# All of TensorE's work in one written order: wide and narrow products in twos, the second column pair one unit behind

## The chip, the core and the metric

The kernel runs on one core of a Trainium2 chip. The metric is the device time of one execution, in microseconds (us), shorter being better. The engines that matter are TensorE (PE, matrix products, with its weight loads on a lane of its own, PEld), VectorE (DVE), ScalarE (ACT) and SyncE (SP), whose queue issues nearly all DMAs.

## The reference

A trunk of four residual layers over 256 tokens of width 2048, in float32: a state-space mixer (SSD), a gated FFN, a short gated convolution, and another gated FFN, with an RMS norm ahead of each and one at the end.

```
for i in range(DEPTH):                       # DEPTH = 2
    h = rms_norm(x, mix_norm_w[i])
    x = x + (ssd_mixer(h, ...) if i % 2 == 0 else short_conv_mixer(h, ...))
    h = rms_norm(x, ffn_norm_w[i])
    x = x + conv_ffn(h, ...)                 # (silu(g) * v) @ w_down, (g, v) = conv(h @ w_up)
return rms_norm(x, final_norm_w)
```

The mixer has 8 groups. For a group it needs the columns xs and z of `h @ w_in`, a matrix of decays m (exponentials of differences of a running sum, times the product of C and B), y = m · (dt · xs) + D · xs, then y · silu(z), an RMS norm over the 512 channels of the group, and the product with w_out.

## The kernel before

**Precision.** Every float32 product is made of three products of a reduced type (float32r). A weight w is split into wh = round(w), a cast on ScalarE (L287), and wl = w − wh, a subtraction on VectorE (L288). An activation is split in the same way into the two halves of a tile `hl` (L217, L218): 256 columns of high parts, then 256 of low ones. The **wide** product (L334) multiplies wh with all 512 columns of `hl`, the **narrow** product (L335) multiplies wl with the 256 high ones. In the mixer's xs and bc streams (`one=True`) the wide product is made as two narrow ones (L331, L332), so that all three add into the same 256 columns.

**Units and streams.** All weight matrices are read as a list of units of 2 × 128 rows by 512 columns (512 KB, `plan`). A unit goes through one of 4 `raw` buffers (the DMA) and one of `WB` = 4 pairs of wh and wl. `stream` (L308) takes one set of 512 output columns: for each unit it takes the four 128-column tiles t and for each t the two k, a wide and then a narrow product. Column tiles 0 and 1 add up in one PSUM buffer, 2 and 3 in another (the two column pairs; there are 3 such buffers, `main`). When the last unit is done, `evac(0)` and `evac(1)` take the two buffers out.

**Side work on TensorE.** Small products and transposes go through two further PSUM buffers (`aux`): the transposes of x at the start (L421), those of ten rows of parameters (L149, `turn_params`), the product that gives dt (L513) and the running sums (L547 to L555); for each mixer group cb (L597), the transposes of xs (L630), the y products (L649, L657), the sum over channels for the norm (L194, fed by `one`, L680) and the broadcast of the norm factor (L187); and the same two for each layer's norm.

**Order.** Each engine runs its own list of instructions from front to back. The kernel's code names the work and what depends on what; where an instruction stands in an engine's list is worked out by a scheduler when the kernel is built, except where `pin` keeps instructions in program order (the startup: `x_pair` as a hook inside the first stream).

**Stages in the profiled execution.** The startup and first stream run to 37 us, dt at about 60, the first xs stream from about 67 and the first z stream from 94.5, then seven more mixer groups; SSD output products, the first FFN from about 700, the short convolution from about 1460, the second FFN from about 1830. In the second FFN the products with w_down (L858 to L860) are three wide products of another form; the change doesn't touch them.

Of the kernel before, what the change touches and what calls it, by code (L numbers as in the profile page):

```python
# [8 lines left out]
F32 = mybir.dt.float32  # L9
# [7 lines left out]
P = 128  # L17
# [22 lines left out]
def trunk_kernel(ctx, tc, a, out):  # L40
    nc = tc.nc
    mm = nc.tensor.matmul
# [16 lines left out]
    n_id = [0]  # L59

# [86 lines left out]
    def turn_params(i, rt, n, put=lambda ins: ins):  # L147
        ps = aux()
        put(nc.tensor.transpose(ps[:, :n], rt[:n, :], ident[:n, :n]))  # L149
        put(nc.vector.tensor_copy(prm[i][:, :n], ps[:, :n]))  # L150
# [31 lines left out]
    def bcast_tok(r, dg=None):  # L182

        dg = dg or diag_tok(r)
# [112 lines left out]

    def weight_unit(c0, kc, ahead=WB - 1):

        i = taken[0]  # L300
        assert plan[i][1:] == (c0, kc), (plan[i], c0, kc)
        taken[0] += 1
        while len(units) < min(i + ahead + 1, len(plan)):
            load_unit()
        got, units[i] = units[i], None
        return got

    def stream(c0, hls, kcs, evac, one=False, before=None):  # L308
# [6 lines left out]
        put = (lambda ins: ins) if before is None else pin  # L315
        for u in range(0, n, KU):
            order = [(t, k) for t in range(4) for k in range(KU)]
            if before is not None and u == 0:
                before(0)
                order.sort(key=lambda tk: tk[1])  # L320
            wh, wl = weight_unit(c0, kcs[u], WB - 1 if before is None else 0)
            for at, (t, k) in enumerate(order):
                if before is not None and at == (0 if u else 2) and u + KU < n:
                    before(u // KU + 1)
                i = u + k
                o = pts[t // 2][:, t % 2, :]
                hl = hls[i // 2][:, i % 2, :]
                lw = slice(t * P, (t + 1) * P)
                first, last = i == 0, i == n - 1
                if one:  # L330
                    put(mm(o[:, 0:T], wh[:, k, lw], hl[:, 0:T], start=first, stop=False))  # L331
                    put(mm(o[:, 0:T], wh[:, k, lw], hl[:, T : 2 * T], start=False, stop=False))  # L332
                else:
                    put(mm(o, wh[:, k, lw], hl, start=first, stop=False))  # L334
                put(mm(o[:, 0:T], wl[:, k, lw], hl[:, 0:T], start=False, stop=last))  # L335
        if before is not None:
            before(n // KU)
        if taken[0] < len(plan):
            while len(units) < min(taken[0] + WB - 1, len(plan)):
                load_unit()  # L340
# [36 lines left out]
    class Norm:  # L377
# [15 lines left out]
        def row(self):  # L393
            one = small.tile([P, T], F32, tag="nacc1", name=uid("nacc1"))
            tt(out=one, in0=self.acc[:, 0, :], in1=self.acc[:, 1, :], op=ALU.add)
            r = mean_rsqrt(tok_sum(one), D)
            ps = bcast_tok(r)
            rb = small.tile([P, T], F32, tag="rrow", name=uid("rrow"))
            nc.scalar.copy(rb, ps)
            return rb  # L400
# [7 lines left out]
    def x_pair(m):  # L408
        if m == NKD // 2:
            for i in range(1, 4):  # L410
                turn_params(i, *prows[i - 1], pin)
            ps = bcast_tok(first["r_tok"], first["dg"])
# [3 lines left out]
            return  # L416
        ps = aux()
        for j in range(2):
            for c in range(2):
                k = 2 * m + j  # L420
                pin(nc.tensor.transpose(  # L421
                    ps[:, j * T + c * P : j * T + (c + 1) * P], xt[:, c, k * P : (k + 1) * P], ident
                ))
        if m:
            load_unit()
        t = xpool.tile([P, 2, T], F32, tag="x", name=uid("x"))
        copy = nc.vector.tensor_copy if m < 2 else nc.scalar.copy
        pin(copy(t, ps.rearrange("p (j t) -> p j t", j=2)))
        xp.append(t)
        h = new_hl()  # L430
        xhl.append(h)
        if m == 0:
            turn_params(0, *prow0, pin)
# [22 lines left out]
    def bc_stream(g, o, before=None):  # L456
# [10 lines left out]
        stream(2 * DI + o * NG * DS + g * DS, xhl, range(NKD), evac, True, before)  # L467
# [42 lines left out]
    ps = aux()  # L510
    for c in range(2):
        for k in range(NKD):
            mm(  # L513
                ps[:, c * NH : (c + 1) * NH], xp[k // 2][:, k % 2, c * P : (c + 1) * P],
                dtw[:, k, :], start=(k == 0), stop=(k == NKD - 1),
            )
    NT = 2 * NH

    def st(tag):
        return tokpool.tile([P, NT], F32, tag=tag, name=tag, bufs=1)  # L520

    v, e, t1, t2, q_ = st("dt_v"), st("dt_e"), st("dt_t1"), st("dt_t2"), st("dt_q")
    for c in range(2):
        stt(
            out=v[:, c * NH : (c + 1) * NH], in0=ps[:, c * NH : (c + 1) * NH],
            scalar=r_tok[:, c : c + 1], in1=bias_bc, op0=ALU.mult, op1=ALU.add,
        )
    na = tokpool.tile([P, NH], F32, tag="na", name="na", bufs=1)
    pin(act(na, alog_bc, AF.Exp))
    act(e, v, AF.Abs)  # L530
    act(e, e, AF.Exp, scale=-1.0)
    ts(out=t1, in0=e, scalar1=2.0, scalar2=None, op0=ALU.add)
    nc.vector.reciprocal(t1, t1)
    tt(out=t1, in0=t1, in1=e, op=ALU.mult)
    tt(out=t2, in0=t1, in1=t1, op=ALU.mult)
    ts(out=q_, in0=t2, scalar1=1.0 / 17.0, scalar2=None, op0=ALU.mult)
    for k in (15, 13, 11, 9, 7, 5, 3):
        stt(out=q_, in0=q_, scalar=1.0 / k, in1=t2, op0=ALU.add, op1=ALU.mult)
    stt(out=q_, in0=q_, scalar=1.0, in1=t1, op0=ALU.add, op1=ALU.mult)
    ts(out=v, in0=v, scalar1=0.0, scalar2=None, op0=ALU.max)  # L540
    dt = cpool.tile([P, 2, NH], F32, tag="dt", name="dt")
    stt(out=dt.rearrange("p c h -> p (c h)"), in0=q_, scalar=2.0, in1=v, op0=ALU.mult, op1=ALU.add)
    da = tokpool.tile([P, 2, NH], F32, tag="da", name="da", bufs=1)
    for c in range(2):
        stt(out=da[:, c, :], in0=dt[:, c, :], scalar=-1.0, in1=na, op0=ALU.mult, op1=ALU.mult)
    ps = aux()
    mm(ps[:, 0:NT], triu, da.rearrange("p c h -> p (c h)"), start=True, stop=True)  # L547
    cs = cpool.tile([P, 2, NH], F32, tag="cs", name="cs")
    nc.vector.tensor_copy(cs.rearrange("p c h -> p (c h)"), ps[:, 0:NT])
    ps = aux()  # L550
    mm(ps[:, 0:NH], ones, da[:, 0, :], start=True, stop=True)
    rem = cpool.tile([P, NH], F32, tag="rem", name="rem")
    tt(out=rem, in0=ps[:, 0:NH], in1=cs[:, 0, :], op=ALU.subtract)
    ps = aux()
    nc.tensor.transpose(ps[:, 0:P], cs.rearrange("p c h -> p (c h)"), ident)  # L555
    cst = tokpool.tile([P, P], F32, tag="cst", name="cst", bufs=1)
    nc.scalar.copy(cst, ps[:, 0:P])
    cs_d = dpool.tile([2, NH, P], F32, tag="cs_d", name="cs_d")
    nc.scalar.dma_start(out=cs_d.rearrange("c h l -> (c h) l"), in_=cst)
# [353 lines left out]
```

## Time and profile before

| | us |
|---|---|
| median of 3 runs | 2562.86 (2562.57 to 2566.78) |
| the profiled execution, whole | 2563.32 |
| its span in the profile | 2561.5 |
| ACT busy | 1321.5 (52%) |
| weight loads (PEld) busy, beside PE | 2235.2 (87%) |

Busy times of PE, DVE, ACT and PEld overlap each other. The row of a matrix product gives a duration that includes its passage through the array, and one product starts long before the one ahead has ended. So the pace of TensorE is read from start to start, or from the count of products in a stretch without idle time, and not from the mean duration. In brackets behind a row stands the idle time of the engine just ahead of it, and what ended it. The granted TensorE clock of the whole execution was 0.998 of full speed. The DMA engines moved 187 GB/s on the mean.

### The profile page before, as it was taken

The numbers are of one execution on the slowest core, as the hardware profiler recorded it, in microseconds if no ns is written. First come the engines' busy times: TensorE is split into PE (matmuls) and PEld (weight loads), VectorE is DVE, ScalarE is ACT, GpSimd is POOL, SyncE is SP. The second block draws the span as 40 slices with busy tenths as digits, with TensorE's granted clock in tenths as the row PEclk, the third lists the DMA queues.
The fourth block names the chain that finished last, engine by engine and source line by source line (L and its number), as shares of the span: only waits on it lengthen the run. The fifth ranks groups of instructions, "written<-read, shape, count | busy, mean of one in ns | idle before, by whom it ended". The sixth has DMA issues, their size and how long they took to land.

```text
span 2561.5 us, 38324 instructions
## 1 busy us (share of the span) xinstructions
PE 2544.6 (99%) x15101; PEld 2235.2 (87%) x15101; DVE 1790.2 (70%) x2601; ACT 1321.5 (52%) x1630; POOL 1.1 (0%) x8
## 2 busy tenths in 40 slices
PE   9999999999999999999999999999999999999998
PEld 9999998998888888888888888888888888888886
DVE  7888876788677776557776666666677774577765
ACT  5565643566555554345554444444555553455543
POOL 0000000000000000000000000000000000000000
PEclk9999999999999999999999999999999999999999
DMA  7666655665666665666665666666566666666664
GB/s 229 175 184 193 182 176 188 189 182 172 198 183 191 190 188 181 193 188 183 193 190 181 193 186 185 185 197 189 174 183 187 189 197 190 193 186 188 189 192 145
DMA packets 255737, 478.76 MB, mean 187 GB/s; under 512 B 17668, under 2 KB 29124, under 8 KB 255428
## 3 DMA queue, kind: packets, MB, share of 16 engines
q1 hardware_dynamic: 254643, 474.13, 61.3%
q8 instruction: 118, 1.93, 0.3%
q10 hardware_dynamic: 912, 2.18, 0.2%
q14 instruction: 64, 0.52, 0.1%
HBM read 474.09 MB, written 2.16 MB: 186 GB/s over the span
## 4 chain that ended last, share of the span: by engine, by line
PE 98%; DVE 1%; ACT 1%; DMA 0%; issue 0%; SPq 0%; DVEq 0%; ACTq 0%
PE main L334 50%; PE main L335 29%; PE main L331 3%; PE main L332 3%; PE main L858 3%; PE main L859 3%; PE main L860 3%; PE aux L649 1%; DVE wl L288 0%; PE aux L657 0%; DMA bias_bc<-in_ssd_dt_bias_dram 0%; PE aux L513 0%; PE aux L630 0%; DMA raw<-in_ssd_w_in_dram 0%; ACT wh L287 0%; PE aux L187 0%
## 5 line engine op out<-in xcount | busy, mean ns | idle before, releaser
L334 PE MATMUL main<-hl,wh 128*128 128x512 f32 x5568 | 1944.9, 396 | 0.2 <-DVE hl L218 0.2
L335 PE MATMUL main<-hl,wl 128*128 128x256 f32 x6336 | 1749.2, 281 | 1.8 <-DVE wl L288 1.8
L288 DVE TENSOR_TENSOR wl<-raw,wh 128x1024 fp32r<-128x1024 f32 (+1 forms) x881 | 1072.6, 1221 | 702.2 <-ACT wh L287 701.6
L287 ACT CAST wh<-raw 128x1024 fp32r<-128x1024 f32 (+1 forms) x881 | 920.8, 1048 | 1067.7 <-PE main L334 735.2
L334 PEld LDWEIGHTS main<-hl,wh 128*128 128x128 f32 x5568 | 1034.8, 188 | 236.7 <-issue 2.0
L335 PEld LDWEIGHTS main<-hl,wl 128*128 128x128 f32 x6336 | 1196.9, 189 | 17.6 <-DVE wl L288 2.7
L331 PE MATMUL main<-hl,wh 128*128 128x256 f32 x768 | 219.5, 287 | 2.5 <-DVE tp L354 1.3
L332 PE MATMUL main<-hl,wh 128*128 128x256 f32 x768 | 218.6, 285 | 0.0
L331 PEld LDWEIGHTS main<-hl,wh 128*128 128x128 f32 x768 | 148.2, 193 | 4.0 <-issue 2.0
L332 PEld LDWEIGHTS main<-hl,wh 128*128 128x128 f32 x768 | 148.3, 193 | 1.5 <-issue 1.1
L858 PE MATMUL main<-wh,hl 128*128 128x512 f32 x352 | 137.5, 391 | 0.8 <-DVE xtok L864 0.8
L859 PE MATMUL main<-wl,hl 128*128 128x512 f32 x352 | 137.4, 390 | 0.0
L860 PE MATMUL main<-wh,hl 128*128 128x512 f32 x352 | 137.0, 389 | 0.0
L370 DVE SCALAR_TENSOR_TENSOR tp<-tp,prm,tp 128x255 f32<-128x255 f32 x208 | 90.6, 477 | 0.0
L346 ACT COPY tp<-main 128x512 f32<-128x512 f32 x128 | 74.3, 580 | 26.0 <-PE main L335 26.0
L348 DVE TENSOR_TENSOR tp<-main,tp 128x512 f32<-128x512 f32 x128 | 87.4, 683 | 0.0
L858 PEld LDWEIGHTS main<-wh,hl 128*128 128x128 f32 x352 | 66.1, 188 | 15.3 <-DVE xtok L864 1.2
L860 PEld LDWEIGHTS main<-wh,hl 128*128 128x128 f32 x352 | 66.1, 188 | 14.2
L859 PEld LDWEIGHTS main<-wl,hl 128*128 128x128 f32 x352 | 66.1, 188 | 13.6
L370 DVE SCALAR_TENSOR_TENSOR g<-tp,prm,g 128x254 f32<-128x254 f32 (+1 forms) x176 | 74.6, 477 | 0.1
L368 ACT ACTIVATE g<-tp,prm,prm 128x256 f32<-128x256 f32 x88 | 48.2, 596 | 38.0 <-DVE tp L357 38.0
L357 DVE TENSOR_TENSOR tp<-tp,rrow 128x512 f32<-128x512 f32 x96 | 66.0, 688 | 1.8
(134 smaller groups left out, 966.9 us busy)
## 6 DMA issues: line engine op xcount, KB each, us to landing
raw<-in_ffn_w_up_dram SPq DMA_DIRECT2D x352, 512.0 KB, 3.7
raw<-in_ffn_w_down_dram SPq DMA_DIRECT2D x176, 512.0 KB, 4.1
raw<-in_ssd_w_in_dram SPq DMA_DIRECT2D x159, 512.0 KB, 4.5
raw<-in_sc_w_in_dram SPq DMA_DIRECT2D x96, 512.0 KB, 4.1
raw<-in_ssd_w_out_dram SPq DMA_DIRECT2D x64, 512.0 KB, 4.2
raw<-in_sc_w_out_dram SPq DMA_DIRECT2D x32, 512.0 KB, 4.2
cbc<-cs_d SPq DMA_DIRECT2D x32, 256.0 KB, 5.1
xt<-in_x_dram SPq DMA_DIRECT2D x8, 256.0 KB, 7.4
```

The source lines that it names most:

```text
L287: put(nc.scalar.copy(wh[:, ks, :], raw[:, ks, :]))
L288: put(tt(out=wl[:, ks, :], in0=raw[:, ks, :], in1=wh[:, ks, :].bitcast(F32), op=ALU.subtract,))
L331: put(mm(o[:, 0:T], wh[:, k, lw], hl[:, 0:T], start=first, stop=False))
L332: put(mm(o[:, 0:T], wh[:, k, lw], hl[:, T : 2 * T], start=False, stop=False))
L334: put(mm(o, wh[:, k, lw], hl, start=first, stop=False))
L335: put(mm(o[:, 0:T], wl[:, k, lw], hl[:, 0:T], start=False, stop=last))
L346: nc.scalar.copy(pb, pt[:, :, T : 2 * T])
L348: tt(out=s, in0=pt[:, :, 0:T], in1=pb, op=ALU.add)
L370: stt(out=y[:, j, d:T], in0=s[:, j, 0 : T - d], scalar=pcol(wname, (width - 1 - d) * nk + k0 + j), in1=y[:, j, d:T], op0=ALU.mult, op1=ALU ...
L858: mm(pt[:, c, :], hi_, wh[:, k, :], start=(i == 0), stop=False)
L859: mm(pt[:, c, :], hi_, wl[:, k, :], start=False, stop=False)
L860: mm(pt[:, c, :], lo_, wh[:, k, :], start=False, stop=(i == n - 1))
```

## The change

Five things change; what is computed stays.

1. Each matrix product and transpose is tied to the one ahead of it in the code (`follow`), so TensorE's list is the order of the code. The side work is handed to the streams as hooks `(step, function)` and runs in the list just ahead of the unit of that step. DVE, ACT and SP are still ordered by the scheduler.
2. Inside a unit and a column tile, the wide products of both k come first, then both narrow ones.
3. The second column pair takes unit u−1 while the first takes unit u. A stream has one step more, and a unit's wh and wl are held for a step longer.
4. The places of the side work: the y products of a group at steps 1, 1, 1 and 3 of the next xs stream, decays and cb at step 4, the channel sum of the norm at step 6; the broadcast and split at step 3 of the z stream, the xs transposes at its step 6. Parameter rows 1 to 3 are transposed right behind the first stream, the last six together at step 5 of the first z stream.
5. At the start, the split of x reads the transposed x from PSUM (`xps`), and the copy of x to SBUF comes behind it; the transpose of parameter row 0 stands ahead of those of x; one more warming product is made.

```diff
+    def follow(inst):
+        if last_pe[0] is not None:
+            tc.add_manual_dep(
+                inst.ins, last_pe[0],
+                mybir.DependencyInfo(
+                    mybir.DependencyClass.NoSync, mybir.DependencyReason.DATA
+                ),
+                reason="stream order",
+            )
+        last_pe[0] = inst.ins.name
+        return inst
...
-        for u in range(0, n, KU):
-            order = [(t, k) for t in range(4) for k in range(KU)]
...
+        def half(p, u):
+            wh, wl = held[u]
+            for t in (2 * p, 2 * p + 1):
...
+                for i, k, hl in part:
+                    if one:
+                        for c in (0, T):
+                            mm(
+                                o[:, 0:T], wh[:, k, lw], hl[:, c : c + T],
+                                start=(i == 0 and c == 0), stop=False,
+                            )
+                    else:
+                        mm(o, wh[:, k, lw], hl, start=(i == 0), stop=False)
+                for i, k, hl in part:
+                    mm(o[:, 0:T], wl[:, k, lw], hl[:, 0:T], start=False, stop=(i == n - 1))
+
+        for step in range(n // KU + 1):
+            u = step * KU
+            for s, fn in hooks:
+                if s == step:
+                    fn()
+            if u < n:
+                held[u] = weight_unit(c0, kcs[u], WB - 2)
+                half(0, u)
+            if u:
+                half(1, u - KU)
+            load_ahead(WB - 1)
         for p in range(2):
             evac(p, pts[p])
...
-        split_pair(h, t, "mix", 2 * m, pin)
+        split_pair(h, xps, "mix", 2 * m, pin)
         if m == 0:
             half(slice(1, 2), pin)
+        t = xpool.tile([P, 2, T], F32, tag="x", name=uid("x"))
+        copy = nc.vector.tensor_copy if m < 2 else nc.scalar.copy
+        pin(copy(t, xps))
+        xp.append(t)
...
+    def after_group(g):
+        return [
+            (1, bind(y_part, g, 0, 0)), (1, bind(y_part, g, 0, 1)), (1, bind(y_part, g, 1, 0)),
+            (3, bind(y_part, g, 1, 1)),
+        ]
...
+        hooks = [(6, bind(tokens_part, g - 1))] if g % 4 else []
...
+        if g == 0:
+            hooks += [(7, make_cs), (8, turn_cs)]
+        else:
+            hooks += [(4, bind(decay_part, g))]
+            if g not in (4, 5):
+                hooks += after_group(g - 1)
+        G[g]["xs"] = xs_stream(g, hooks)
...
+        elif g == 0:
+            hooks = [(1, bind(decay_part, 0)), (5, last_params), (7, turned)]
+        else:
+            hooks = [(3, bind(split_part, g - 1)), (6, turned)]
+        G[g]["zs"] = z_stream(g, hooks)
...
+        [(0, s - (s == 3), fn) for s, fn in after_group(NG - 1)]
+        + [(0, 4, last_group(tokens_part)), (0, 6, last_group(split_part))],
```

How this moves instructions is shown at three places. The first is TensorE's list in an up stream of the first FFN. `main_…` is the PSUM buffer of a column pair, `hl_…` the activation, `wh_…` and `wl_…` the two parts of one unit; 512 or 256 at the end is the width. Before, around the step from one unit to the next:

```order
L335 MATMUL main_9658<-hl_7752,wl_9750 128x256
L334 MATMUL main_9867<-hl_7148,wh_9771 128x512
L335 MATMUL main_9867<-hl_7148,wl_9772 128x256
L334 MATMUL main_9867<-hl_7148,wh_9771 128x512
L335 MATMUL main_9867<-hl_7148,wl_9772 128x256
```

Now, at such a place:

```order
L75 MATMUL main_11980<-hl_7545,wl_12015 128x256 x2
L75 MATMUL main_11980<-hl_7545,wh_12014 128x512 x2
L75 MATMUL main_11980<-hl_7545,wl_12015 128x256 x2
L75 MATMUL main_11981<-hl_7357,wh_11992 128x512 x2
L75 MATMUL main_11981<-hl_7357,wl_11993 128x256 x2
```

Wide and narrow products came in turn and come in twos now, and the second buffer (`main_11981`) takes another unit (`wh_11992`) than the first (`wh_12014`): the one that the first had a step ago. (All products have the line of the helper `mm` now, L75, and all transposes that of `turn`, L78.)

The second place is VectorE's list in the xs stream of the second mixer group, around the sum `nacc` (the tile `one`) that TensorE's channel sum waits for. `cb` and `decay` belong to the second group, `yg`, `tp` and `nacc` to the norm of the first; `wl` are the weight splits. Before, the stretch around `nacc`, and one that comes 25 rows later:

```order
L674 TENSOR_TENSOR yg_1328<-yg_1328,z_1528 128x512
L288 TENSOR_TENSOR wl_1751<-raw_1748,wh_1750 128x1024
L678 TENSOR_TENSOR tp_1532<-tp_1532,tp_1535 128x512
L680 TENSOR_TENSOR nacc_215_1538<-tp_1532 128x256
L288 TENSOR_TENSOR wl_1781<-raw_1778,wh_1780 128x1024
```

```order
L600 TENSOR_TENSOR cb_1580<-aux_1577,mask_101 128x384
L288 TENSOR_TENSOR wl_1978<-raw_1975,wh_1977 128x1024
L288 TENSOR_TENSOR wl_2000<-raw_1997,wh_1999 128x1024
L618 TENSOR_TENSOR decay_1584<-decay_1584,cb_1580 128x768
L618 TENSOR_TENSOR decay_1595<-decay_1595,cb_1580 128x768
L618 TENSOR_TENSOR decay_1606<-decay_1606,cb_1580 128x768
```

Now:

```order
L735 TENSOR_TENSOR yg_1541<-yg_1541,z_1505 128x512
L664 TENSOR_TENSOR cb_1645<-aux_1642,mask_101 128x384
L306 TENSOR_TENSOR wl_1639<-raw_1636,wh_1638 128x1024
L682 TENSOR_TENSOR decay_1649<-decay_1649,cb_1645 128x768
L682 TENSOR_TENSOR decay_1660<-decay_1660,cb_1645 128x768
L682 TENSOR_TENSOR decay_1671<-decay_1671,cb_1645 128x768
L739 TENSOR_TENSOR tp_1752<-tp_1752,tp_1755 128x512
L306 TENSOR_TENSOR wl_1718<-raw_1715,wh_1717 128x1024
L741 TENSOR_TENSOR nacc_245_1758<-tp_1752 128x256
```

One `cb` and three `decay` multiplications, which stood behind the sum, stand ahead of it now.

The third place is step 5 of the first z stream. TensorE's list before, at two of the four points where parameter rows were transposed (`prow`, into `aux`):

```order
L149 MATMUL aux_688<-ident,prow_686 128x128
L334 MATMUL main_1340<-hl_192,wh_1190 128x512
L149 MATMUL aux_694<-ident,prow_691 128x128
```

```order
L149 MATMUL aux_700<-ident,prow_697 128x128
L334 MATMUL main_1339<-hl_301,wh_1343 128x512
L149 MATMUL aux_705<-ident,prow_703 128x128
```

TensorE's list now, and then VectorE's around the copies that empty these `aux` buffers:

```order
L75 MATMUL main_1222<-hl_296,wl_1234 128x256 x2
L78 MATMUL aux_1377<-ident,prow_1374 128x128
L78 MATMUL aux_1382<-ident,prow_1380 128x128
L78 MATMUL aux_1388<-ident,prow_1385 128x128
L78 MATMUL aux_1394<-ident,prow_1391 128x128
L78 MATMUL aux_1399<-ident,prow_1397 128x128
L78 MATMUL aux_1404<-ident,prow_1402 128x32
L75 MATMUL main_1221<-hl_380,wh_1326 128x512 x2
```

```order
L306 TENSOR_TENSOR wl_1349<-raw_1346,wh_1348 128x1024
L682 TENSOR_TENSOR decay_1255<-decay_1255,cb_1240 128x768
L169 COPY prm_126<-aux_1377 128x128
L169 COPY prm_127<-aux_1382 128x128
L306 TENSOR_TENSOR wl_1371<-raw_1368,wh_1370 128x1024
L682 TENSOR_TENSOR decay_1266<-decay_1266,cb_1240 128x768
L169 COPY prm_128<-aux_1388 128x128
L169 COPY prm_129<-aux_1394 128x128
L169 COPY prm_130<-aux_1399 128x128
L169 COPY prm_131<-aux_1404 128x32
```

The six transposes stand in one run now, while there are two `aux` buffers, and the copies that free them stand between weight splits and decays.

More of the change, by code (lines that the diff above doesn't have):

```diff
@@ L335, in stream @@
[L335 to L340, printed above, removed]
+                mm(o, wh[:, k, lw], hl[:, 0:T], start=(i == 0), stop=False)
+                mm(o, wh[:, k, lw], hl[:, T : 2 * T], start=False, stop=False)
+                mm(o, wl[:, k, lw], hl[:, 0:T], start=False, stop=(i == n - 1))
@@ L557, in trunk_kernel @@
[L557 to L570 removed]
+    NT = 2 * NH
+    dt = cpool.tile([P, 2, NH], F32, tag="dt", name="dt")
```

370 lines of the change are left out of this document (200 added, 170 removed).

## The prediction

> **What bounds the kernel now.** I read the page's first part (busy time), then the chain that ended last, then the costliest groups.
>
> ```profile
> PE 2544.6 (99%) x15101; PEld 2235.2 (87%) x15101; DVE 1790.2 (70%) x2601; ACT 1321.5 (52%) x1630; POOL 1.1 (0%) x8
> PE 98%; DVE 1%; ACT 1%; DMA 0%; issue 0%; SPq 0%; DVEq 0%; ACTq 0%
> L334 PE MATMUL main<-hl,wh 128*128 128x512 f32 x5568 | 1944.9, 396 | 0.2 <-DVE hl L218 0.2
> L335 PE MATMUL main<-hl,wl 128*128 128x256 f32 x6336 | 1749.2, 281 | 1.8 <-DVE wl L288 1.8
> L288 DVE TENSOR_TENSOR wl<-raw,wh 128x1024 fp32r<-128x1024 f32 (+1 forms) x881 | 1072.6, 1221 | 702.2 <-ACT wh L287 701.6
> ```
>
> TensorE is busy throughout and is the chain itself: before its 5568 wide and 6336 narrow products it idles 2.0 us in all. There is hardly a stall to take away, so only two things can move the time: the pace of the products when nothing waits, and new stalls. VectorE idles 702.2 us ahead of its weight splits, waiting for casts: over the whole span it has slack. How it stands in the mixer is another matter, below.
>
> **The pace.** Products in a long FFN stretch, in two short pieces (first and last wide product of each, with 6 and 9 between them), and in an all-wide and an all-narrow stretch:
>
> ```profile
> L334 PE MATMUL main<-hl,wh 128*128 128x512 f32 x2053 | 715.5, 396 | 0.0
> ...
> 999.71 0.40 PE L334 MATMUL main<-hl,wh 128*128 128x512 f32 x1
> ...
> 1002.14 0.39 PE L334 MATMUL main<-hl,wh 128*128 128x512 f32 x1
> ...
> 1032.93 0.40 PE L334 MATMUL main<-hl,wh 128*128 128x512 f32 x1
> ...
> 1036.47 0.40 PE L334 MATMUL main<-hl,wh 128*128 128x512 f32 x1
> ...
> 2459.98 0.39 PE L858 MATMUL main<-wh,hl 128*128 128x512 f32 x1
> ...
> 2461.34 0.39 PE L858 MATMUL main<-wh,hl 128*128 128x512 f32 x1
> ...
> 137.90 0.28 PE L331 MATMUL main<-hl,wh 128*128 128x256 f32 x1
> ...
> 142.34 0.28 PE L332 MATMUL main<-hl,wh 128*128 128x256 f32 x1
> ```
>
> The first row is of the 720 us from 720 to 1440: 0.3507 us for each pair of a wide and a narrow product. The two pieces give (1002.14 − 999.71)/7 = 0.347 and (1036.47 − 1032.93)/10 = 0.354: the same order has a faster and a slower pace. A wide product between wide ones takes (2461.34 − 2459.98)/6 = 0.227, a narrow one between narrow ones (142.34 − 137.90)/37 = 0.120.
>
> The trace has no two wide, two narrow products in a row. Bounds: put together from the all-wide and all-narrow paces, two pairs take 2·0.227 + 2·0.120 = 0.694 instead of 0.701, so 0.347 a pair, as in the fast piece; 5568 pairs save 5568·0.0037 = **20 us**. At the slow piece's pace they lose 5568·0.0033 = **18 us**. In between, unchanged: 0. As the slow and fast paces already share out the present order, and the paces of like products point to the fast one, I take half of the gain, **−10 us**.
>
> The Trainium skill ("TensorE: Matmul & The Clock Gate", section "Back-to-back issue gap") has a gap of N/2.4 + 2.5 ns, 216 for a wide and 109 for a narrow product, 0.325 a pair, which would give 143 us if the new order brought it about. The trace doesn't agree even where wide follows wide: 0.227.
>
> **The lag of the second pair.** It lets TensorE leave the first buffer 2.8 us before the second, but the three buffers hardly cost a wait so far (idle 0.2 before L334), so it gains nothing. It holds wh and wl a step (8 pairs, 2.8 us) longer. In the FFN and the convolution I leave that at 0, because VectorE idles ahead of the splits there; gone, that cover would cost up to one wl (1.2 us) for each of the streams.
>
> **The start.** Startup rows of PE, ACT and DVE:
>
> ```profile
> 6.15 0.69 DVE L428 COPY x<-aux 128x512 f32<-128x512 f32 x1 [4.10 <-PE aux L421]
> ...
> 7.53 0.58 PE L331 MATMUL main<-hl,wh 128*128 128x256 f32 x1 [1.18 <-ACT hl L217]
> ...
> 38.71 0.38 PE L335 MATMUL main<-hl,wl 128*128 128x256 f32 x1 [1.36 <-DVE wl L288]
> ...
> 40.42 1.05 ACT L287 CAST wh<-raw 128x1024 fp32r<-128x1024 f32 x1 [0.46 <-DMA raw<-in_ssd_w_in_dram]
> ...
> 41.51 1.23 DVE L288 TENSOR_TENSOR wl<-raw,wh 128x1024 fp32r<-128x1024 f32 x1 [0.28 <-ACT wh L287]
> 42.65 0.48 DVE L150 COPY prm<-aux 128x128 f32<-128x128 f32 x2
> ...
> 46.33 0.35 PE L331 MATMUL main<-hl,wh 128*128 128x256 f32 x1 [1.28 <-DVE tp L354]
> ```
>
> Reading x from PSUM takes the copy (0.69 us at 6.15) off the path to the first product at 7.53: −0.65. Behind the first stream, at about 36.8, the third parameter transpose now stands ahead of the whole next stream and needs an `aux` buffer that the copies at 42.65 free; VectorE still has these behind four splits, the last of them held up by a DMA (the cast waits for `raw` at 40.42). TensorE idles from 36.8 to about 42.8, 6 us, where it had only the stalls of 1.4 (38.71) and 1.3 (46.33) before: 6 − 2.7, so **+3 us** net (0 if the DMAs land earlier, 5 if the clock drops).
>
> Before, no gap behind 13 us is longer than 1.4 us, so the trace shows no clock drop. The Trainium skill (the same page, Part 1) halves the clock after an idle window of about 3.4 us; with this rule the 6 us gap would add some 2 us, the upper bound.
>
> **The first z stream.** Rows of ACT (cst), SP (cbc) and DVE:
>
> ```profile
> 94.24 0.27 ACT L557 COPY cst<-aux 128x128 f32<-128x128 f32 x1 [2.15 <-PE aux L555]
> ...
> 97.84 0.88 SPq L606 DMA_DIRECT2D cbc<-cs_d  x2
> ...
> 103.24 0.29 DVE L610 TENSOR_SCALAR decay<-cbc,cs 128x128 f32<-128x128 f32 x1 [3.07 <-DMA cbc<-cs_d]
> ...
> 114.86 0.55 DVE L600 TENSOR_TENSOR cb<-aux,mask 128x384 f32<-128x384 f32 x1
> 115.44 2.70 DVE L618 TENSOR_TENSOR decay<-decay,cb 128x768 f32<-128x768 f32 x3
> ```
>
> The running sums reach the decays through a write and a read of DRAM, 9 us from the copy to the first decay; VectorE waits 3.07 us for it. Queued behind this wait are eleven small rows (about 2.6 us) and then a weight split that the stream needs at step 4, due at about 94.5 + 3.5·2.8 = 104.3. It ends at 103.24 + 2.6 + 1.2 = 107 then: **3 us** of stall (0 to 4). At step 5 six transposes share two `aux` buffers. From that split to the sixth copy VectorE has three further splits (1.2 each), three decay multiplications (0.9) and small rows for some 4 us: about 10 to 11 us for which TensorE has one step (2.8) and part of the transposes to do. I take **6 us** of stall (0 to 9, since VectorE may have run ahead): 9 us together.
>
> **The channel sums.** In the second group's xs stream, which begins at 119.89 (the last three rows are of lists over wider stretches: all engines from 120 to 168, and the y products in one group):
>
> ```profile
> 119.89 0.28 PE L331 MATMUL main<-hl,wh 128*128 128x256 f32 x1
> ...
> 133.95 1.22 DVE L288 TENSOR_TENSOR wl<-raw,wh 128x1024 fp32r<-128x1024 f32 x1 [1.90 <-ACT wh L287]
> 135.42 1.22 DVE L288 TENSOR_TENSOR wl<-raw,wh 128x1024 fp32r<-128x1024 f32 x1 [0.24 <-ACT wh L287]
> ...
> 140.97 0.42 DVE L680 TENSOR_TENSOR nacc<-tp 128x256 f32<-128x256 f32 x1
> ...
> 142.46 0.50 PE L194 MATMUL aux<-ones,nacc 128*128 128x1 f32 x4
> ...
> 120.00:168.00 48.00, 48.00 (x354) 43.86 (x353) 45.34 (x94) 30.94 (x39) 0.00 (x0) 1.00 0.68 190
> ...
> L649 PE MATMUL aux<-decay,xdt 128*64 128x256 f32 x16 | 2.5, 392 | 0.0
> L657 PE MATMUL aux<-decay,xdt 128*64 128x128 f32 x16 | 1.6, 279 | 0.0
> ```
>
> The hook stands ahead of step 6, with 5.5 units of 24 narrow products (15.8 us) ahead of it and the y products and cb (4.1 us of busy time for the y products, which overlap; about 3.7 with cb): TensorE is there at about 139.4. The sum it waits for ended at 141.39 before, 2.0 us later; TensorE did other products until 142.46, which its fixed list forbids now. Ahead of the sum VectorE newly has cb (0.55) and three decay multiplications (2.70); its 2.14 us of idle time at 133.95 and 135.42 can take some of it. 2.0 + 3.25 − 2.14 = **3.1 us** of stall. Bounds: 5.2 if the idle time stays, 0.3 if the first pair's evacuation, 2.8 us earlier now, helps VectorE as much. Groups 2, 3, 4, 7 and 8 have this hook behind such a list: 5·3.1 = **15.5 us** (1.5 to 26). Everything on PE stands behind it.
>
> **The last group.** Its norm and split now stand in the output stream, steps 4 and 6, the split right ahead of the unit that needs it:
>
> ```profile
> 642.36 0.50 PE L334 MATMUL main<-hl,wh 128*128 128x512 f32 x1 [0.22 <-DVE hl L218]
> ```
>
> Before, TensorE lost 0.22 there; I take **+2 us** (0 to 4, a broadcast and split's length).
>
> **Sum**, against the profiled execution's 2563.32 (2561.5 of span and 1.8 around it; the median shown is 0.5 lower): −0.65 + 3 + 9 + 15.5 + 2 − 10 = +19, so **2582**.
>
> **The rivals.**
>
> *Faster: the pace wins and VectorE keeps up.* A bare 0.347 us a pair gives −20, and the lag, which starts each evacuation 2.8 us earlier, puts the sums in time (1.5), with the z stream at 3 and the start at 2.4: 2563.3 − 13 = **2550**. For it: the all-wide pace, and VectorE's 30% of free time. Against it: in the mixer VectorE is nearly full, busy 45.34 (the third figure) of the 48 us from 120 to 168. It turns on the sum `nacc` being ready about 19.5 us into an xs stream, and on pairs under 0.3485. Chance 0.30.
>
> *A draw.* About 10 us of stalls against 10 us of pace: **2563**. Chance 0.12.
>
> *The pace loses.* The new order falls into the slow piece's 0.354 (+18) beside 29 us of stalls: **2610**. For it: the slow pace exists in this trace, with the same products. Chance 0.08.
>
> *It doesn't do what it says.* The lag frees buffers that nobody waited for, and the pace stays: the stalls alone, 2563.3 + 29 = 2592, which lies in the forecast's own range.
>
> **How the numbers follow.** Forecast 2582 (its own range 2570 to 2602: the sum with −20 and with 0 of pace, and somewhat more stall), chance 0.50. With the rivals: faster by over 0.2% (about what a measurement of this kernel can tell from no change, 5 us) 0.30, within it 0.12, slower 0.58. The range has to reach to the faster rival: **2543 to 2602** leaves out about 2 in 10, the deep end of the fast side and the slow rival.
>
> **What would show it.** In the profile after: idle time ahead of the channel sums, waiting for `nacc`, some 3 us in each of five groups (none: the faster rival); one gap of about 6 us at 37 waiting for a `prm` copy; idle time ahead of the parameter transposes in the first z stream; and the count of wide products from 720 to 1440, 2053 before: 2075 is the fast pace, 2034 the slow. The prediction is wrong if the FFN, over half of the run, shows a pace outside these bounds, or if stalls appear in it, as wl is held longer.

## The result and the profile after

The changed kernel takes 2606.34 us (median of 4 runs, 2604.73 to 2609.64), the kernel before 2563.51: a ratio of 1.0166, 95% interval 1.0149 to 1.0184. It is 43 us slower. The forecast was 2582, slower by 19; the direction holds, and the time lies above the range that ended at 2602.

The page of the changed kernel, first the busy times, then the chain that ended last:

```profile
PE 2545.6 (98%) x15103; PEld 2235.6 (86%) x15103; DVE 1799.9 (69%) x2601; ACT 1332.8 (51%) x1634; POOL 1.1 (0%) x8
...
PE 92%; DVE 2%; ACT 1%; issue 0%; ACTq 0%
```

TensorE is busy as long as before (2544.6), in a span that is 41 us longer, and its share of the chain fell from 98% to 92%. So TensorE waits. For what it waits is in the view of waits, TensorE's alone: the waiting line and tile, who was waited for, us in all, times, the longest.

```profile
PE aux L75 <- DVE yg L726: 19.2, 8, 3.6
PE aux L78 <- DVE prm L169: 8.3, 3, 6.2
PE aux L75 <- DVE nacc L741: 5.9, 5, 2.0
PE aux L78 <- DMA cbc<-cs_d: 4.7, 1, 4.7
PE main L75 <- DVE hl L236: 3.3, 2, 2.9
PE main L75 <- DVE wl L306: 1.5, 1, 1.5
```

The first row was not in the forecast: eight times, once in each mixer group, a y product waits for VectorE's addition `yg` of the y product ahead of it. Timeline of TensorE in the second of these places (start, duration, line, then the idle time before it):

```profile
198.46 0.87 PE L75 MATMUL aux<-decay,xdt 128*64 128x256 f32 x8
201.52 1.52 PE L75 MATMUL aux<-decay,xdt 128*64 128x256 f32 x16 [2.18 <-DVE yg L726]
```

The products of two halves j go into one PSUM buffer. In the code before, the products of both stood ahead of both additions; now `y_part` makes product, addition, product, addition, and the second product may not write the buffer while the first addition has not read it.

The stalls have an after-effect. Stretches of the changed kernel around the first of the y gaps (us, then the five engines' busy time and counts, the granted TensorE clock, DMA share, GB/s):

```profile
140.00:142.00 2.00, 1.06 (x11) 0.54 (x9) 0.79 (x1) 1.67 (x3) 0.00 (x0) 1.00 0.62 141
142.00:144.00 2.00, 0.00 (x0) 0.00 (x0) 2.00 (x8) 0.00 (x0) 0.00 (x0) 0.77 0.58 163
144.00:146.00 2.00, 1.34 (x9) 0.96 (x11) 1.21 (x4) 1.70 (x2) 0.00 (x0) 0.50 0.68 235
146.00:148.00 2.00, 2.00 (x12) 1.29 (x11) 1.54 (x4) 1.97 (x3) 0.00 (x0) 0.50 0.44 96
...
150.00:152.00 2.00, 2.00 (x19) 2.00 (x19) 1.15 (x6) 1.99 (x4) 0.00 (x0) 1.00 0.39 87
```

After 3.6 us without work the clock is at half, and twelve products fit into 2 us; from 150 to 152, at full clock, it is nineteen. While it lasts TensorE counts as busy, so that this loss shows in no row of the waits. It can be estimated as TensorE's busy time times the missing part of the clock: windows of 1 us from 20 to 760 us sum to 9.8 us in the profiled run of the changed kernel, and to nothing in the kernel before. One of its four stretches at half clock (627.6 to 634.4) stands behind a gap of only 2.00 us. TensorE's row there, and its windows (PE busy, then the clock):

```profile
627.76 0.97 PE L75 MATMUL aux<-ones,nacc 128*128 128x1 f32 x4 [2.00 <-DVE nacc L741]
```

```profile
626.00:628.00 2.00, 0.24 (x2) 0.95 0.11 44
628.00:630.00 2.00, 2.00 (x10) 0.50 0.73 194
```

The start, of which the forecast expected 0.65 us, went the other way. ScalarE's and VectorE's rows in a middle pair of the first stream, and the first parameter transpose behind that stream, before:

```profile
28.48 0.91 ACT L217 ACTIVATE hl<-x,prm 128x256 fp32r<-128x256 f32 x2
29.02 0.89 DVE L218 SCALAR_TENSOR_TENSOR hl<-x,prm,hl 128x256 fp32r<-128x256 f32 x2
...
36.73 0.38 PE L149 MATMUL aux<-ident,prow 128*128 128x128 f32 x2
```

Now, with the gap that follows:

```profile
24.08 0.48 DVE L236 SCALAR_TENSOR_TENSOR hl<-aux,prm,hl 128x256 fp32r<-128x256 f32 x1
24.59 0.47 ACT L235 ACTIVATE hl<-aux,prm 128x256 fp32r<-128x256 f32 x1 [1.32 <-DVE hl L236]
25.10 0.48 DVE L236 SCALAR_TENSOR_TENSOR hl<-aux,prm,hl 128x256 fp32r<-128x256 f32 x1 [0.54 <-ACT hl L235]
...
40.88 0.38 PE L78 MATMUL aux<-ident,prow 128*128 128x128 f32 x2
...
47.42 0.47 PE L78 MATMUL aux<-ident,prow 128*128 128x128 f32 x1 [6.17 <-DVE prm L169]
```

The two engines take turns at the buffer: VectorE 24.08, ScalarE 24.59, VectorE 25.10. Before, with x in SBUF, each did its two halves in one go (0.91 and 0.89 us), partly side by side. The first stream ends 4.15 us later for it (40.88 against 36.73), and behind it comes the gap of 6.17 that the forecast had as 6.

### The profile page after: what moved, and what is told of

Read it like the earlier page. It is cut to its first block, busy times and chain, and to the rows that moved or that the text cites. A ratio compares the mean times of both kernels' runs of the same rounds, so it can differ in the third digit from the quotient of the medians.

```text
span 2602.9 us, 38337 instructions
## 1 busy us (share of the span) xinstructions
PE 2545.6 (98%) x15103; PEld 2235.6 (86%) x15103; DVE 1799.9 (69%) x2601; ACT 1332.8 (51%) x1634; POOL 1.1 (0%) x8
## 3 DMA queue, kind: packets, MB, share of 16 engines
q10 hardware_dynamic: 912, 2.18, 0.2%
## 4 chain that ended last, share of the span: by engine, by line
PE 92%; DVE 2%; ACT 1%; issue 0%; ACTq 0%
PE main L75 90%; PE aux L75 1%; DVE wl L306 1%; PE aux L78 0%; DVE decay L682 0%; ACT wh L305 0%; DVE tp L401 0%; DVE yg L726 0%; DVE decay L674 0%; DVE decay L676 0%; DVE decay L678 0%; DVE tp L739 0%; DVE nacc L741 0%; ACT z L652 0%; DVE xtok L983 0%
## 5 line engine op out<-in xcount | busy, mean ns | idle before, releaser
L75 PE MATMUL main<-hl,wh 128*128 128x512 f32 (+1 forms) x7104 | 2014.1, 373 | 4.9 <-DVE hl L236 3.3
L75 PEld LDWEIGHTS main<-hl,wl 128*128 128x128 f32 x6336 | 1170.2, 189 | 249.0 <-DVE wl L306 1.9
L75 PE MATMUL main<-hl,wl 128*128 128x256 f32 x6336 | 1256.4, 279 | 1.5 <-DVE wl L306 1.5
L75 PEld LDWEIGHTS main<-hl,wh 128*128 128x128 f32 x7104 | 1066.3, 190 | 12.8 <-DVE hl L236 7.8
L75 PE MATMUL main<-wh,hl 128*128 128x512 f32 x704 | 217.7, 390 | 0.8 <-DVE xtok L983 0.8
L75 PEld LDWEIGHTS main<-wh,hl 128*128 128x128 f32 x704 | 132.2, 188 | 29.5 <-DVE xtok L983 1.2
L75 PE MATMUL main<-wl,hl 128*128 128x512 f32 x352 | 137.5, 391 | 0.0
L75 PEld LDWEIGHTS main<-wl,hl 128*128 128x128 f32 x352 | 66.1, 188 | 13.5
L421 ACT ACTIVATE tp<-tp,prm,prm 128x256 f32<-128x256 f32 x88 | 48.0, 593 | 0.0
L75 PE MATMUL aux<-decay,xdt 128*64 128x256 f32 (+1 forms) x256 | 27.4, 348 | 19.2 <-DVE yg L726 19.2
L423 DVE SCALAR_TENSOR_TENSOR xs<-tp,prm,xs 128x253 f32<-128x253 f32 (+2 forms) x96 | 40.8, 475 | 0.7 <-ACT xs L421 0.7
L75 PEld LDWEIGHTS aux<-decay,xdt 128*64 128x64 f32 x256 | 16.3, 142 | 28.3 <-DVE yg L726 21.1
L682 DVE TENSOR_TENSOR decay<-decay,cb 128x768 f32<-128x768 f32 x32 | 29.3, 951 | 10.7 <-ACT decay L680 10.6
L866 ACT ACTIVATE g<-g 128x512 f32<-128x512 f32 x44 | 27.9, 633 | 16.6 <-DVE g L423 13.9
```

Of the source, the lines that this page charges most:

```text
L75: return follow(nc.tensor.matmul(*args, **kw))
L421: act(y[:, j, :], s[:, j, :], AF.Identity, bias=pcol(bname, k0 + j), scale=w)
L423: stt(out=y[:, j, d:T], in0=s[:, j, 0 : T - d], scalar=pcol(wname, (width - 1 - d) * nk + k0 + j), in1=y[:, j, d:T], op0=ALU.mult, op1=ALU ...
L682: tt(out=mf, in0=mf, in1=cb.rearrange("p j l -> p (j l)").unsqueeze(1).to_broadcast([P, 2, 3 * P]), op=ALU.mult,)
L866: act(y, y, AF.Silu)
```

## The experiments

Twelve kernels ran; medians of their timed runs, in brackets the ratio to the kernel before on the same chip, with its 95% interval. The kernel before had a median of 2565.41 us in the first round (e1 to e4), 2563.16 in the second (e5 to e8) and 2563.84 in the third (e10 to e13), so that a difference between kernels of two rounds is sure to some 2 us only. Diffs are against the kernel named; `...` marks lines left out.

**One stall at a time, on the changed kernel.** The y products (the additions of the first column pair behind both products):

```diff
-        stt(
-            out=y[:, j, :], in0=xs[pr][:, j, :],
...
-        )
+        for i in ((), (0, 1))[j] if pr == 0 else (j,):
+            stt(
+                out=y[:, i, :], in0=xs[pr][:, i, :],
...
+            )
```

> The changed kernel with one edit: the two yg additions of a group's first column pair come behind the y products of both its halves, as before the change, so that the second half's products no longer wait for VectorE to read the PSUM buffer that both halves share. Theory A (each stall is a matter of its own place): the eight gaps of 2.45 to 3.9 us between the first and second half's y products go, and with the first of them 3.4 us at half clock (1.7 us): 22 + 1.7, so about 2582 us, and the waits for nacc stay at 1.1 to 1.3 us each. Rival B (VectorE is behind in the mixer, and TensorE meets it at the next wait): the y gaps go but the waits for nacc grow by as much as the y gaps were, 2.4 us each in five groups, so about 2594 us.

Measured: 2605.58 us, no gain (ratio to before 1.0158, 1.0143 to 1.0173). The y waits are gone, and those for `nacc` have grown from 5.9 to 18.9 us. The view of waits of e1_y, and VectorE's list ahead of one `nacc` with TensorE's row that waits for it:

```profile
PE aux L75 <- DVE nacc L742: 18.9, 5, 4.1
```

```profile
213.42 0.55 DVE L664 TENSOR_TENSOR cb<-aux,mask 128x384 f32<-128x384 f32 x1
213.88 1.21 DVE L306 TENSOR_TENSOR wl<-raw,wh 128x1024 fp32r<-128x1024 f32 x1
215.02 2.69 DVE L682 TENSOR_TENSOR decay<-decay,cb 128x768 f32<-128x768 f32 x3
217.62 0.68 DVE L740 TENSOR_TENSOR tp<-tp,tp 128x512 f32<-128x512 f32 x1
218.23 2.35 DVE L306 TENSOR_TENSOR wl<-raw,wh 128x1024 fp32r<-128x1024 f32 x2
220.50 0.41 DVE L742 TENSOR_TENSOR nacc<-tp 128x256 f32<-128x256 f32 x1
...
221.05 0.98 PE L75 MATMUL aux<-ones,nacc 128*128 128x1 f32 x4 [3.71 <-DVE nacc L742]
```

In these rows VectorE works without a break up to `nacc`, with cb and three decays ahead of it: rival B of this run. Theory A, by which each stall is a matter of its own place, falls for the mixer. The time lies nearly 12 us above rival B's too. The y products and `nacc` waited 25.1 us together in the changed kernel and 18.9 here, but windows of 1 us lose 19.8 us at half clock here against 9.8: fewer and longer gaps, and more of them with a clock drop. e5_y_dec shows the same from the other side.

The x split from the SBUF copy, which stands ahead of it again:

```diff
+        pin(copy(t, xps))
...
-        split_pair(h, xps, "mix", 2 * m, pin)
+        split_pair(h, t, "mix", 2 * m, pin)
...
-        pin(copy(t, xps))
```

> The changed kernel with one edit: the split of x at the start reads the copy of x in SBUF again, not the PSUM buffer. Theory A: ScalarE's and VectorE's parts of the split take turns when both read one PSUM buffer and lie side by side when they read SBUF, so the pairs of gaps of 0.36 and 0.52 us at each x pair go and the first stream ends at about 37 us instead of 41.0: about 2602 us. Rival B: the startup waits for its DMAs, and the end of the first stream stays within 1 us of 41: 2606 us.

Measured: 2605.31 us (1.0159, 1.0144 to 1.0174). The number is rival B's, the start is theory A's: the parameter transpose's gap came to its end 4.7 us earlier (42.74 instead of 47.42). What it won was lost again at half clock. The mean granted clock of its four runs is 0.991, of the changed kernel's 0.993, and windows of 1 us lose 19.7 us in its profiled run, which was the slowest of the four (2609.56), against 9.8. One of these stretches stands behind a later y gap, in TensorE's rows and the clock of e2_x (PE busy, then the clock):

```profile
310.54 2.05 PE L75 MATMUL aux<-decay,xdt 128*64 128x256 f32 x16 [2.18 <-DVE yg L726]
```

```profile
310.00:312.00 2.00, 1.46 (x14) 0.85 0.87 237
312.00:314.00 2.00, 2.00 (x13) 0.50 0.47 151
```

The same gap of 2.18 us, at 201.52 in the changed kernel, left the clock at 1.00 in the 2 us behind it, and so did the one at 254.90 in e2_x itself. The half clock falls on some of these gaps and not on others, so a kernel full of gaps is no place to measure 5 us.

The two last weight splits behind the copies of the parameters:

```diff
                 turn_params(i, *prows[i - 1], pin)
+            for _ in range(2):
+                load_unit()
...
-            for _ in range(2):
-                load_unit()
```

> The changed kernel with one edit: the last two weight splits that the first stream loads ahead are issued behind the three parameter transposes and their copies instead of ahead of them. Theory A: the copies, and not the transposes, held TensorE; without splits ahead of them that wait for a DMA the gap of 6.4 us behind the first stream shrinks to under 1.5 us, the half clock behind it (47.4 to 51) goes, and the next stream waits some 1 to 2 us for its second weight split: 2606 - 5 - 1.8 = about 2600 us. Rival B: the next stream's weight splits come from the same late DMA, so that the wait only moves into the stream and 1 us at most is won: 2605 us, with one gap of 4 us or more and the half clock as before.

Measured: 2604.32 us (1.0154, 1.0138 to 1.0169). The 6.17 us gap is 1.6 us, as theory A had it, but the gain is the 2 us of rival B; windows of 1 us lose 14.8 us at half clock in its profiled run, against 9.8. The six late transposes, spread:

```diff
...
-            hooks = [(1, bind(decay_part, 0)), (5, last_params), (7, turned)]
+            hooks = [(1, bind(decay_part, 0)), (7, turned)]
+            hooks += [(s, bind(last_param, i)) for s, i in zip((2, 3, 4, 5, 6, 6), range(4, nrt))]
```

> The changed kernel with one edit: the six last parameter transposes stand one at a step (two at the last) at steps 2 to 6 of the first z stream instead of all at step 5. Theory A: the gaps of 4.7 and 1.9 us came from six transposes through two PSUM buffers and VectorE's copies between long work; spread out, each finds its buffer free: both gaps go with 1.7 us of half clock, the gap of 1.5 us for wl stays: 2606 - 8 = about 2598 us. Rival B: VectorE is late there by the wait for the decay rows (3.45 us for cbc), so TensorE waits elsewhere in the same stream, for copies or weight splits, and no more than 3 us are won: about 2603 us.

Measured: 2601.13 us (1.0138, 1.0121 to 1.0155), 5 us won, between the two theories.

**VectorE's list.** The kernel of e1_y, with cb and the decays back in the z stream:

```diff
-            hooks += [(4, bind(decay_part, g))]
+            if g == 4:
+                hooks += [(4, bind(decay_part, g))]
...
-            hooks = [(3, bind(split_part, g - 1)), (6, turned)]
+            hooks = [(3, bind(split_part, g - 1)), (4, bind(decay_part, g)), (6, turned)]
```

> The kernel of e1_y with one more edit: cb and the decays of groups 2, 3, 4, 6, 7 and 8 are hooked to step 4 of the group's z stream (where VectorE did them before the change) instead of step 4 of its xs stream, so that VectorE's list has no cb and no decay multiplication ahead of nacc. Theory B (VectorE reaches nacc late because 3.25 us of cb and decays stand ahead of it; the y gaps were the same lateness, met earlier): the waits for nacc, 18.9 us in e1_y, fall under 3 us: 2605.6 - 17 = about 2588 us. Rival C (VectorE is late at nacc by its whole load in a group, wherever cb and the decays stand): the waits for nacc stay above 10 us or come back in the z stream ahead of weight splits or the xs transposes: 2600 us or more.

Measured: 2575.27 us (1.0045, 1.0033 to 1.0058): 30.3 us less than e1_y (28.1 when each is set against the kernel before of its round), more than either theory gave. No wait for `nacc` is left. Of the 30.3, 18.9 are these waits. The other 11 stand in no row of the waits; they are of the size of five stretches at half clock. Behind each of the five gaps, of 3.7 to 4.1 us, windows of 1 us lose 1.7 to 3.1 us in e1_y, 12.2 in sum, and e5_y_dec has no such stretch there. The edit was not run on the changed kernel with its order of the y products, so what the decays alone are worth there is not shown. The clock in e1_y behind the `nacc` gap at 221, and in e5_y_dec in a like place:

```profile
220.00:224.00 4.00, 2.95 (x14) 2.98 (x15) 2.52 (x12) 0.00 (x0) 0.00 (x0) 0.50 0.74 242
224.00:228.00 4.00, 4.00 (x26) 4.00 (x26) 0.88 (x6) 1.05 (x1) 0.00 (x0) 0.70 0.05 20
```

```profile
208.00:212.00 4.00, 4.00 (x36) 4.00 (x35) 2.43 (x7) 1.81 (x2) 0.00 (x0) 1.00 0.87 273
212.00:216.00 4.00, 4.00 (x36) 4.00 (x34) 3.27 (x11) 1.05 (x1) 0.00 (x0) 1.00 0.81 271
```

**The pace.** The changed kernel with wide and narrow products in turn, and the kernel before with the twos:

```diff
                 for i, k, hl in part:
                     ...
                         mm(o, wh[:, k, lw], hl, start=(i == 0), stop=False)
-                for i, k, hl in part:
                     mm(o[:, 0:T], wl[:, k, lw], hl[:, 0:T], start=False, stop=(i == n - 1))
```

> The changed kernel with one edit: inside a unit and column tile the wide and narrow products alternate again (the order of the hooks and the lag stay). Theory A (the twos give the faster pace, some 2.3 ns for each of 5568 pairs): about 2606 + 13 = 2619 us, with the stalls of the mixer as they are. Rival B (the pace comes from the lag or from where the tiles lie, not from the twos): 2606 us.

```diff
+            if before is None:
+                for t in range(4):
...
+                    for i, k, hl in part:
...
+                        else:
+                            mm(o, wh[:, k, lw], hl, start=(i == 0), stop=False)
+                    for i, k, hl in part:
+                        mm(o[:, 0:T], wl[:, k, lw], hl[:, 0:T], start=False, stop=(i == n - 1))
+                continue
             for at, (t, k) in enumerate(order):
```

> The kernel before with one edit: in all streams but the first both wide products of a column tile come ahead of both narrow ones; the scheduler sets the order as before, there is no lag and no hook. Theory A (the pace is the twos' alone, and nothing else in the change is needed for it): 2563.5 - 13 = about 2551 us. Rival B (the pace needs the fixed order, or the scheduler's freedom breaks the twos up): 2563 us.

Measured: e6_turn 2639.01 us (1.0291, 1.0277 to 1.0305), e7_before_twos 2550.68 (0.9951, 0.9937 to 0.9964). The twos alone, in the kernel before and under its scheduler, win 12.5 us, as theory A had it, and this version beats both kernels. The rows of the wide products from 800 to 1440 us, of e6_turn, of the changed kernel and of e7_before_twos; their count is the pace:

```profile
L75 PE MATMUL main<-hl,wh 128*128 128x512 f32 x1827 | 640.7, 397 | 0.0
```

```profile
L75 PE MATMUL main<-hl,wh 128*128 128x512 f32 x1838 | 576.9, 395 | 0.0
```

```profile
L332 PE MATMUL main<-hl,wh 128*128 128x512 f32 x1839 | 575.9, 395 | 0.0
```

Pairs in turn come at 640/1827 = 0.3503 us, twos at 0.348. The first is a mean of two paces: from 850 to 1000 us e6_turn makes 433 pairs (0.346), from 1100 to 1400 it makes 850 (0.353); the changed kernel makes 431 and 863 there, 0.348 both times. So the twos are no faster than the turn at its best; they keep one pace where the turn falls into a slower one.

e6_turn lost 33 us against the changed kernel where theory A had 13. Its products in turn are no slower than before on the mean of this stretch (the kernel before has 1827 too), but they are in the short convolution: from 1540 to 1780 its row has 681 wide products, where the changed kernel has 690 and the kernel before 687. Not all of the 33 is pace: windows of 1 us lose 18.6 us at half clock in its profiled run, against 9.8. Why the turn is slower in the convolution than in the kernel before was not found out.

**What is left, on a quiet kernel.** All mendings together: e5_y_dec with the edits of e2_x, e3_params and e4_z0, and the first group's decays at step 5 of the first z stream:

> The kernel of e5_y_dec with the startup and first z stream mended too: the split of x from the SBUF copy (as e2_x), the two last weight splits behind the parameter copies (e3_params), the six parameter transposes at steps 2 to 6 (e4_z0), and the first group's cb and decays at step 5 of the first z stream instead of step 1. Theory B: what is left of the stalls is some 2 us behind the first stream, 2 to 4 us in the first z stream, under 3 us for nacc, 3 us in the last group, against a pace gain of 13: 2563.5 - 13 + 9 = about 2560 us. Rival C (VectorE stays the limit of the mixer in a fixed order): stalls of 15 us and more stay, 2572 us or more.

Measured: 2562.59 us (0.9998, 0.9989 to 1.0007), as theory B had it. And each of the three alone on e5_y_dec, where the mixer has hardly a gap left:

> The kernel of e5_y_dec, which has hardly a gap left in the mixer, with one edit: the split of x reads the copy in SBUF (as e2_x on the changed kernel). In e2_x the first stream ended 4.7 us earlier and the whole gained nothing, with more half clock behind gaps of 2.3 to 2.5 us. Theory A (the 4.7 us are real and the half clock, which falls by chance on such gaps, hid them): 2575.3 - 4.5 = about 2571 us. Rival B (what the first stream gains is waited for again in the first streams behind it): 2575 us.

> The kernel of e5_y_dec with one edit: the two last weight splits ahead of the first stream's end stand behind the parameter copies (as e3_params). In e3_params the gap of 6.4 us shrank to 1.9 us. Theory A: 4.5 us of gap and 1.8 us of half clock go, 0.7 us comes back as a wait for a weight split: about 2570 us. Rival B: as in e3_params 2 us at most are won: 2573 us.

> The kernel of e5_y_dec with one edit: the six parameter transposes of the first z stream at steps 2 to 6, one at a step, and the first group's cb and decays at step 5 instead of 1. Theory A: of the gaps of 2.3, 3.35 and 2.7 us and 3.3 us of half clock (1.7 us lost), 2 to 5 us of a wait for a parameter row's DMA or copy stay: about 2569 us. Rival B: VectorE's and the queue's wait for the written and re-read running sums holds TensorE all the same: 2574 us or more.

Measured: 2569.84, 2570.48 and 2571.85 us (ratios 1.0022, 1.0026 and 1.0029): 5.4, 4.8 and 3.4 us won, 13.6 in sum, beside 12.7 for all together (e8_all). The first two are theory A's; the same edits had won 1 and 2 us on the changed kernel. In the third, TensorE still waits 5.8 us for the DMA of a parameter row, between theory A and B.

The lag taken out of e8_all:

```diff
                 half(0, u)
-            if u:
-                half(1, u - KU)
+                half(1, u)
```

> The kernel of e8_all with one edit: both column pairs take the same unit again (no lag); twos, hooks and the fixed order stay. Theory A (the lag frees buffers that nobody waits for; the pace is the twos'): no change beyond 3 us, 2560 to 2566. Rival B (in a fixed order the lag hides the evacuation of the streams, or feeds VectorE 2.8 us earlier): waits for tp or z copies or for nacc appear, 2570 us or more. Rival C (the lag slows the pace, as the alternating order with the lag was slower than the same order before): the FFN goes faster by 1 to 2 ns a pair, 2552 to 2557 us.

Measured: 2571.69 us (1.0028, 1.0018 to 1.0039), 9.1 us slower than e8_all (8.4 when each is set against the kernel before of its round): the time of rival B. Of the waits that rival B named one shows. Its view of waits has 3.0 us where e8_all has 1.4, for the evacuation of the first stream:

```profile
PE main L75 <- DVE tp L406: 3.0, 1, 3.0
```

Behind this gap the clock is at half, and windows of 1 us from 41 to 49 lose 2.7 us, which e8_all doesn't lose there. All of TensorE's waits together are 19.8 us against 16.7. The rest is spread in losses too short for this view; in the FFN from 800 to 1440 it does 1832 pairs, e8_all 1838. So the lag pays once the order is fixed; that it does so by hiding evacuations is shown for this one wait only.

## Why the prediction was right and wrong

The direction and most of the mechanisms held, the size did not: 43 us where 19 were forecast. The term that failed first is the mixer's, +15.5. It counted waits for `nacc` at 3.1 us each and put the half clock behind such waits at nothing; the mixer cost 30.3 us (e1_y against e5_y_dec; in the trace of the changed kernel, 25.1 us of waits and 6.0 of half clock). The second is the split of x, −0.65, which cost 5.4.

**The pace, −10: right.** Measured −12.5 (e7_before_twos), between unchanged and the fast bound of −20. From 720 to 1440 us the changed kernel makes 2065 wide products, between the 2053 of before and the 2075 of the fast pace, and none of them waited. That half of the gain was taken was a choice between bounds, so that it came near is luck; the reason, two paces of which the twos avoid the slow one, was half seen in the two pieces of the trace.

**The channel sums, +15.5: the mechanism right, the step of the sum wrong.** That cb and the decays stand ahead of `nacc` and that TensorE may not pass it was read from the list, and e5_y_dec shows it. The step that failed is "2.0 + 3.25 − 2.14 = 3.1 us", in two ways. VectorE's idle time of 2.14 was credited in full against the new work. In e1_y, in the same stream (TensorE's first product of it at 140.14), VectorE idles 1.65 us at 142.68, 0.69 at 150.79 and 0.44 at 154.42, all ahead of cb (156.94), and not at all from there to `nacc`, so the new work could not use it. `nacc` ends at 164.44, 24.3 us into the stream, where it was 21.5 before: 2.8 later, and 1.1 was forecast. The five waits were 18.9/5 = 3.8 us each. And the step stops at the wait: the half clock behind the five waits, some 12 us in e1_y, is the larger part of what was missing. In the changed kernel itself 19.2 us of the lateness were met earlier, by the y products, and 5.9 at `nacc`.

**The y products: missing.** The forecast counted their time and not the new order of product and addition in a shared buffer. By e1_y this wait cost nothing on top of the sum: without it the waits for `nacc` and the half clock behind them took its place.

**The half clock: weighed at one place only.** The forecast let the clock drop behind the gap of the start, as an upper bound of 2 us (1.8 by windows of 1 us). Its own 3 us stalls in the mixer were not asked the same question. Mending them gave 30.3 us for 18.9 us of `nacc` waits. The Trainium skill ("TensorE: Matmul & The Clock Gate", Part 1) has a free-running window of about 3.4 us. The trace agrees: the stretches at half clock last 3.4 us (311.2 to 314.6 in e2_x), twice that (143.0 to 149.8 in the changed kernel) or, once, three times that (118.0 to 128.4 in e12_quiet_params), and each gap of 3.6 us and more in the traces here has one. It adds that gaps of 2.00 and 2.18 us can have one too.

**The split of x, −0.65: the sign wrong.** What failed is the view that reading PSUM takes only the copy away. Read from PSUM, ScalarE's and VectorE's halves take turns; undone, it gives 5.4 us (e11_quiet_x).

**The start, +3, and the first z stream, +9: about right.** Mending the first gave 4.8 us with its half clock (e12_quiet_params). In the z stream the gaps were 1.48, 4.69 and 1.87, 8.0 in all, and the mending took away 3.4, with a wait for a DMA in the place of the others.

**The last group, +2: right in kind,** 2.9 us of wait for hl.

**The lag, 0: wrong, in the other direction.** It is worth 9.1 us in the mended kernel. That "the three buffers hardly cost a wait" held for a scheduler that fills each wait with other work, and not for a fixed list, is the likely reason; e10_nolag shows it for one wait of 3.0 us.

Taken together, from the trace of the changed kernel: the start 4.15 + 6.17 − 2.7 (the two stalls of before) + 1.8 of half clock = 9.4; the first z stream 8.0 + 2.1 of half clock = 10.1; the mixer 19.2 + 5.9 + 6.0 of half clock = 31.1; the last group 2.9; the pace −12.5. That is 41.0 us, where the two spans differ by 41.4. The mended versions give nearly the same, 5.4 + 4.8 for the start and 30.3 for the mixer. The forecast had 2.4, 9, 15.5, 2 and −10. What it lacked is half of what the mixer cost, in waits and in half clock, and the turns of the split.

## What to carry to other kernels

When a free order is replaced by a written one, each wait that other products used to fill becomes idle time, so read for every fixed instruction what stands ahead of its input on the engine that makes it, and credit that engine's idle time only where the new work is ready to use it. Ask of each stall of 2 us and more what the clock does behind it. A stall taken away at one place may be the same lateness of one engine, met at the next place; only moving that engine's work shows it. And a change with two aims is best split: here the order of four products won 0.5% alone, and the rest of the change lost over 2%.

## What was not expected of the hardware

A gap of 2.18 us halved TensorE's clock in one place (0.50 from 312 to 314 us in e2_x) and left it at 1.00 behind the same gap in others; one of 2.00 us halved it in the changed kernel (627.76). Behind the gaps of 3.6 us and more that are shown here it fell to 0.50 each time, and the stretches at half clock last 3.4 us or two or three times that. Two wide and two narrow products come at 0.348 us a pair in every stretch counted here, in turn at 0.346 in one and 0.353 in another; what holds the products in turn back was not found out.
